# Weight splitting in a two-layer hybrid decoder: the exact parts kept in DRAM by the first token group and loaded by the other three

## The chip, the cores and the metric

The kernel runs on one core of one Trainium2 chip. A time is the device time of one execution in microseconds (us). The time before is 2350.82 us, the median of three runs (2337.67 to 2355.39). Lower is better. TensorE is called PE here, VectorE DVE, ScalarE ACT, GpSimd POOL, and SyncE, which issues the DMAs, SP, as in the profile.

## The reference

The reference is one inference step of a two-layer decoder for 16 meta tokens and 2048 prompt tokens, and for 8 samples of one token each, with a model width of 1024, all in 32-bit floats.

```
# layer 0 (AB): sliding-window attention and gated DeltaNet side by side
h = _rmsnorm(x, norm_g)
proj = jnp.einsum('btd,de->bte', h, w_in)             # 1024 -> 3336
...
mix = jnp.concatenate([oa, ob.reshape(Bn, T, B_VAL)], axis=-1)
y = x + jnp.einsum('bte,ed->btd', mix, w_out)         # 1024 -> 1024
# layer 1 (C): gated linear attention
h = _rmsnorm(x, norm_g)
proj = jnp.einsum('btd,de->bte', h, w_in)             # 1024 -> 3088
...
y = x + jnp.einsum('bte,ed->btd', o.reshape(Bn, T, C_VAL), w_out)
```

Then comes one last RMSNorm. The step also gives back the caches and the states of both layers. Most of the work are the four products of all tokens with weight matrices.

## The kernel before, in words

**Precision.** A 32-bit number is written as the sum of two parts that PE multiplies exactly in its faster format (float32r): `hi` is the rounded number, `lo` is the rest. A product needs three matmuls: hi with hi, hi with lo, lo with hi. Tokens and weights are both taken apart in this way.

**Groups.** The tokens are worked off in four groups (`NGROUPS`): group 0 has the 8 samples, the 16 meta tokens and 512 prompt tokens (536 columns, in two halves of 268), the others have 512 prompt tokens each. Every group goes through both layers, and so every group uses all the weights once. The head of the next group (`ab_head`) is put ahead of the last product of layer C of the group before (`c_out`).

**Weights.** `load_w` (L234) brings one weight tile: SP loads it from DRAM into a tile `raw` (L239), ACT (L244) or, for layer C's values, DVE (L246) writes `hi` into a tile `wh`, and POOL subtracts to give `lo` in a tile `wl` (the subtraction shows under the helper's line L111). A tile of over 512 columns is split in two pieces. There are two buffers of `raw`, three of `wh` and three of `wl`. This is done in each of the four groups anew. `proj` (L370) then multiplies: for each of eight blocks of 128 input features three matmuls of 512 columns (L108), so 24 matmuls for a full weight of 128 x 1024; `proj_tok` (L388) does the same for layer C's values with the tokens as the stationary operand, from two weight tiles at once, and `proj_tok2` (L409) for the attention's values, with both parts side by side in tiles of `wh`. In `c_out` the last group takes the last two feature blocks of the output weights apart in a piece of code of its own (L1205).

**Output products.** `ab_out` multiplies by the first layer's output weights in two passes of eight weight tiles, the first over the features that are ready early (three of eight blocks in the later groups), the second over the rest; each weight of the second pass ends with an addition on DVE and a store to DRAM (L969). `c_out` works in one pass, with a load from DRAM and a store (L1186) for each weight.

**What sets the order.** The program emits the large products (`bulk`) and, between their pieces, steps of the streams of dependent work (attention blocks, the DeltaNet's inverses and scans, norms). An estimated clock with a latency for each step (`DEF_LAT`) says when a stream gets its next step. The instructions then go to the engines' queues; each engine works its queue off in order. A tile's buffer is given to the next tile of its tag when the last reader of the old one is done. All DMAs are issued by SP, in one queue.

Other names in the profile: `pp` are the accumulators of the large products, `pc` those of the streams, `t` any working tile, `inv` the DeltaNet's triangular inverse, `x1d` and `x2d` the residual in DRAM. L114 is the helper for scalar_tensor_tensor on DVE, L118 and L120 those for tensor_scalar, L187 a power on POOL.

Of the kernel before, what the change touches and what calls it, by code (L numbers as in the profile page):

```python
# [9 lines left out]
F32 = mybir.dt.float32  # L10
# [33 lines left out]
def _constants():  # L44
# [9 lines left out]
    # the first level's, transposed  # L54
# [13 lines left out]
def kernel(ctx: ExitStack, tc: tile.TileContext, ins, outs):  # L68
# [12 lines left out]
    def nm(s):  # L81
        cnt[0] += 1
        return f"{s}_{cnt[0]}"
# [47 lines left out]
    UN = 1088  # L131
# [3 lines left out]
    w0 = wp.tile([128, UN], F32, tag="raw", bufs=2, name="raw0")  # L135
# [6 lines left out]
    # The first group's parts are taken before its tokens' scale is known, which then goes to the products.  # L142
# [46 lines left out]
    # W_up, stacked in exact parts  # L189
# [8 lines left out]
    # carried state  # L198
# [15 lines left out]
    # running log decays of the heads as rows, in exact parts, and what picks a head's rows  # L214
    # (the same rows hold layer C's gates in their time)
# [18 lines left out]
    def load_w(src, n, eng):  # L234
        if src is w0:
            raw = w0
        else:
            raw = wp.tile([128, UN], F32, tag="raw", bufs=2, name=nm("raw"))
            SY.dma_start(raw[:, :n], src)  # L239
        hi = wp.tile([128, UN], F32R, tag="wh", bufs=3, name=nm("wh"))  # L240
        lo = wp.tile([128, UN], F32R, tag="wl", bufs=3, name=nm("wl"))
        for w in (slice(0, n // 2), slice(n // 2, n)) if n > 512 else (slice(0, n),):
            if eng == "A":
                A.copy(hi[:, w], raw[:, w])  # L244
            else:
                V.tensor_copy(hi[:, w], raw[:, w])  # L246
            TT(lo[:, w], raw[:, w], hi[:, w].bitcast(F32), sub, G)
        return hi, lo
# [5 lines left out]
    # Streams of dependent work are interleaved with the bulk of the products along an estimated clock (us).  # L254
# [29 lines left out]
    def bulk(gen, hooks=()):  # L284
        # hooks: what to emit at the pieces of the product, counted from its last one
# [14 lines left out]
    # Tiles that live long: a stream asks for room and yields until others have given some back.  # L300
# [69 lines left out]
    def proj(q, src, H, evac, eng="V", kts=tuple(range(8))):  # L370
        # src holds the rows of the input features kts, in that order
        hiX, loX = H
        K = len(kts)
        hi, lo = load_w(src, 128 * K, "A")
# [13 lines left out]
    def proj_tok(q, parts, H, N, windows):  # L388
        hiX, loX = H
        per = 8 // len(parts)  # L390
        hl = [load_w(src, per * N, "V") for src in parts]
# [17 lines left out]
    def proj_tok2(q, src, H, N, windows):  # L409
        # few columns: both parts of the weights side by side in one pass of each part of the tokens  # L410
        raw = wp.tile([128, UN], F32, tag="raw", bufs=2, name=nm("raw"))
        SY.dma_start(raw[:, :8 * N], src)
        ws = []
        for x in range(2):
            w = wp.tile([128, 4, 2, N], F32R, tag="wh", bufs=3, name=nm("wh"))
            r = raw[:, 4 * N * x:4 * N * x + 4 * N].rearrange("p (k m) -> p k m", k=4)
            A.copy(w[:, :, 0], r)
            TT(w[:, :, 1], r, w[:, :, 0].bitcast(F32), sub, G)
            ws.append(w)
        for (slot, c0, evac) in windows:  # L420
# [64 lines left out]
        # sample tokens  # L485
# [36 lines left out]
        # caches of the sample tokens  # L522
# [75 lines left out]
    def ab_proj(q, src, evac):  # L598
        if q.g:
            return proj(q, src, q.H, evac)  # L600
# [5 lines left out]
        return proj(q, src, q.H, ev)  # L606

    def ab_norm(q, ahead):
        # in two steps: the tokens times their scale, ahead of time, then the parts
# [66 lines left out]
    def ab_scalars(q, BA, NS):  # L676
        # token scalars: write strength, log decay and its running sums
# [46 lines left out]
    def ab_k(q):  # L724
# [28 lines left out]
        yield from ab_proj(q, ins["w_ab"][0] if g else w0, ev_k)  # L753
# [9 lines left out]
    def ab_conv(q, h):  # L763
# [23 lines left out]
        for j in range(3):  # L787
# [22 lines left out]
            bulk(ab_proj(q, ins["w_ab"][9 + ct], ev_c))  # L810
# [9 lines left out]
        bulk(ab_proj(q, ins["w_ab"][21 + h], gate(q, G_[0], 4 + h)))  # L820
# [4 lines left out]
    def ab_swa(q, u):  # L825
# [17 lines left out]
        bulk(ab_proj(q, ins["w_ab"][1 + u], ev_q))  # L843
# [4 lines left out]
        bulk(ab_proj(q, ins["w_ab"][5 + u], gate(q, Gt, u)))  # L848
# [80 lines left out]
    def ab_out(q, xs):  # L929
        # output projection, residual; the next layer's input as it comes  # L930
# [903 lines left out]
```

## Time and profile before

| what | value |
|---|---|
| runs, us | 2337.67, 2355.39, 2350.82 |
| span of the profiled execution, first to last instruction | 2346.1 us |
| instructions | 44344 |
| mean granted PE clock | 0.972 |
| read from HBM, written | 192.56 MB, 31.77 MB |
| mean DMA rate over the span | 96 GB/s |

The profile shows one execution. Its own time is given by its span of 2346.1 us alone; the median of the runs is 4.7 us above it. How to read its rows: a group of instructions is named by line, engine, operation and tiles, written tile first (`wl<-raw,wh` is the subtraction that gives `lo`), then the shape and a count; behind the first bar the busy time and the mean duration, behind the second the idle time of the engine ahead of them and who ended it. In a timeline, the first number is the start in us from the span's start, the second the duration; a bracket gives the wait ahead of it and its releaser. The matmuls are pipelined, so that PE's durations overlap. The granted clock is a share of full speed.

### The profile page before, as it was taken

The page shows a single profiled execution, that of the slowest core. Times are in us where ns is not written, and L with a number is a line of the kernel's source. Part 1 is how long each engine was busy: PE and PEld are TensorE (multiplying, and loading weights), DVE is VectorE, ACT ScalarE, POOL GpSimd, SP SyncE. Part 2 cuts the span into 40 slices and gives each one's busy share as a digit, 9 for nine tenths or more (in the row PEclk, how much of TensorE's full clock was granted, in tenths as well). Part 3 has the DMA queues.
Part 4 walks back from the last instruction along what each step waited for, and adds up shares of the span by engine and source line. Part 5 has one row for each costly group of instructions (what it writes and reads, how often), then busy time and mean ns, then how long its engine had stood idle before and what let it go on. Part 6 is the DMA issues. An engine that isn't in the chain of part 4 may idle for free. (4 is left out here: it accounts for less than half of the span.)

```text
span 2346.1 us, 44344 instructions
## 1 busy us (share of the span) xinstructions
PE 2193.5 (93%) x17290; PEld 1834.6 (78%) x17290; DVE 1406.2 (60%) x3708; ACT 1007.8 (43%) x2617; POOL 960.8 (41%) x794
## 2 busy tenths in 40 slices
PE   7898997989999999999999999999999999999998
PEld 6777786988879776778887777778887867778886
DVE  7788974565475666646445666565446475665533
ACT  4444543343463344444444344345344334455333
POOL 2332222444543332345453523255563423254644
PEclk9999998999999999999999999999999999999999
DMA  4221213324533411232333511142323521152223
GB/s 133 81 78 46 64 42 104 107 84 149 171 118 125 161 46 50 83 116 79 107 101 104 184 55 46 53 152 68 109 99 98 163 96 47 35 155 78 84 72 113
DMA packets 108077, 226.15 MB, mean 96 GB/s; under 512 B 15899, under 2 KB 42171, under 8 KB 107851
## 3 DMA queue, kind: packets, MB, share of 16 engines
q1 hardware_dynamic: 107866, 223.31, 30.1%
q8 instruction: 136, 2.23, 0.4%
q14 instruction: 75, 0.61, 0.1%
HBM read 192.56 MB, written 31.77 MB: 96 GB/s over the span
## 5 line engine op out<-in xcount | busy, mean ns | idle before, releaser
L108 PE MATMUL pp<-t,wh 128*128 128x512 f32 (+1 forms) x4528 | 1289.8, 368 | 18.2 <-ACT t L148 8.9
L111 POOL TENSOR_TENSOR wl<-raw,wh 128x512 fp32r<-128x512 f32 (+4 forms) x552 | 702.7, 1292 | 968.1 <-ACT wh L244 808.4
L108 PEld LDWEIGHTS pp<-t,wh 128*128 128x128 f32 x4528 | 794.7, 193 | 132.2 <-issue 13.0
L108 PE MATMUL pp<-t,wl 128*128 128x512 f32 (+1 forms) x2264 | 817.4, 361 | 0.3 <-POOL wl L111 0.3
L108 PEld LDWEIGHTS pp<-t,wl 128*128 128x128 f32 x2264 | 436.1, 193 | 60.3 <-issue 3.2
L244 ACT CAST wh<-raw 128x512 fp32r<-128x512 f32 (+3 forms) x488 | 269.3, 585 | 426.2 <-PE pp L108 178.5
L108 PE MATMUL pp<-wh,t 128*128 128x256 f32 (+1 forms) x1360 | 246.6, 290 | 9.6 <-DVE QKt L111 6.3
L108 PEld LDWEIGHTS pp<-wh,t 128*128 128x128 f32 x1360 | 209.1, 192 | 13.0 <-DVE QKt L111 6.5
L111 POOL TENSOR_TENSOR t<-t,t 128x512 fp32r<-128x512 f32 (+3 forms) x128 | 164.4, 1301 | 122.0 <-ACT t L548 83.1
L114 DVE SCALAR_TENSOR_TENSOR t<-pp,t 128x512 f32<-128x512 f32 (+3 forms) x160 | 92.6, 584 | 124.7 <-PE pp L108 89.2
L187 POOL TENSOR_TENSOR sm<-sm,mh 128x2 f32<-128x2 f32 (+3 forms) x84 | 65.5, 780 | 247.3 <-DVE sm L120 110.2
L108 PE MATMUL pp<-wl,t 128*128 128x256 f32 (+1 forms) x544 | 157.2, 289 | 0.0
L114 DVE SCALAR_TENSOR_TENSOR t<-t,PV,t 128x512 fp32r<-128x512 f32 (+5 forms) x160 | 116.0, 729 | 30.8 <-ACT t L965 22.2
L111 DVE TENSOR_TENSOR t<-t,t 128x512 f32<-128x512 f32 (+4 forms) x103 | 87.4, 852 | 36.0 <-ACT t L367 34.1
L108 PEld LDWEIGHTS pp<-wl,t 128*128 128x128 f32 x544 | 104.9, 193 | 0.7
L114 DVE SCALAR_TENSOR_TENSOR t<-pp,PV,t 128x511 f32<-128x511 f32 (+2 forms) x108 | 79.9, 740 | 17.9 <-ACT t L801 17.8
L108 PEld LDWEIGHTS pc<-t,t 128*128 128x128 f32 (+4 forms) x496 | 64.9, 166 | 29.0 <-ACT t L1462 4.9
L108 PE MATMUL pc<-t,t 128*128 128x128 f32 (+5 forms) x496 | 80.7, 274 | 7.1 <-DVE t L114 4.0
L873 ACT ACTIVATE t<-t,sm 128x257 f32<-128x257 f32 x128 | 64.1, 503 | 29.6 <-DVE sm L114 28.7
L111 DVE TENSOR_TENSOR QKt<-pp,t 128x512 f32<-128x512 f32 (+1 forms) x40 | 23.0, 583 | 87.4 <-PE pp L108 87.4
L114 DVE SCALAR_TENSOR_TENSOR t<-t,t 128x512 f32<-128x512 f32 (+4 forms) x92 | 63.9, 695 | 18.7 <-ACT t L1102 11.7
L111 DVE TENSOR_TENSOR t<-pp,t 128x268 f32<-128x268 f32 (+1 forms) x90 | 44.5, 496 | 49.2 <-PE pp L108 27.0
(336 smaller groups left out, 3006.9 us busy)
## 6 DMA issues: line engine op xcount, KB each, us to landing
raw<-in_w_ab SPq DMA_DIRECT2D x100, 512.0 KB, 3.7
raw<-in_w_c SPq DMA_DIRECT2D x64, 512.0 KB, 3.6
t<-in_xT SPq DMA_DIRECT2D x72, 256.0 KB, 4.0
raw<-in_w_cv SPq DMA_DIRECT2D x24, 512.0 KB, 3.5
raw<-in_w_co SPq DMA_DIRECT2D x24, 512.0 KB, 3.6
out_yp<-t SPq DMA_DIRECT2D x32, 256.0 KB, 2.3
raw<-in_w_abo SPq DMA_DIRECT2D x24, 320.0 KB, 3.2
t<-rows SPq DMA_DIRECT2D x24, 256.0 KB, 4.4
```

The costliest lines, as they stand in the source:

```text
L108: T.matmul(out, lhsT, rhs, start=start, stop=stop)
L111: (eng or V).tensor_tensor(out, a, b, op=op)
L114: V.scalar_tensor_tensor(out, a, s, b, op0=op0, op1=op1)
L187: G.tensor_tensor(out, x, mh[0:x.shape[0]].to_broadcast(list(x.shape)), op=ALU.pow)
L244: A.copy(hi[:, w], raw[:, w])
L873: A.activation(S_[:, kv], S_[:, kv], AF.Exp, bias=st[:, 2 + kv:3 + kv], accum_out=st[:, 4 + kv:5 + kv])
```

## The change

In group 0 a weight is taken apart as before, and both parts are then stored to a DRAM tile of their own (`keep_parts`; the stores are emitted two weights later by `flush`). In groups 1 to 3 `load_w` loads the two parts straight into `wh` and `wl` (`load_parts`), with no work on ACT, DVE or POOL. The same holds for the attention's values (`proj_tok2`) and for the last group's piece in `c_out`. All weight tiles, `raw`, `wh` and `wl` (and `wv`), now share one tag with `NW` = 8 buffers, in place of two, three and three. Each weight gets a name and a column, by which its parts are found again; where the change passes these on (`ab_proj`, the calls of `proj` and `proj_tok`) only arguments differ. Comments are also dropped.

```
+NW = 8
...
+    parts_of = {}
+    unstored = []
+
+    def w_tile(n, dt=F32R):
+        return wp.tile([128, UN], dt, tag="w", bufs=NW, name=nm(n))
+
+    def flush(keep):
+        while len(unstored) > keep:
+            SY.dma_start(*unstored.pop(0))
+
+    def keep_parts(w, n, hi, lo):
+        name, c0 = w
+        if name not in parts_of:
+            parts_of[name] = dr.tile([128, 2, UN], F32, tag=nm("wd"), bufs=1, name=nm("wd"))
+        for x, t in enumerate((hi, lo)):
+            unstored.append((parts_of[name][:, x, c0:c0 + n], t.bitcast(F32)))
+
+    def load_parts(w, n, hi, lo):
+        name, c0 = w
+        flush(0)
+        for x, t in enumerate((hi, lo)):
+            SY.dma_start(t.bitcast(F32), parts_of[name][:, x, c0:c0 + n])
+
+    def load_w(q, w, src, n, eng):
+
+        if q.g:
+            hi, lo = w_tile("wh"), w_tile("wl")
+            load_parts(w, n, hi[:, :n], lo[:, :n])
+            return hi, lo
         if src is w0:
             raw = w0
         else:
-            raw = wp.tile([128, UN], F32, tag="raw", bufs=2, name=nm("raw"))
+            raw = w_tile("raw", F32)
             SY.dma_start(raw[:, :n], src)
-        hi = wp.tile([128, UN], F32R, tag="wh", bufs=3, name=nm("wh"))
-        lo = wp.tile([128, UN], F32R, tag="wl", bufs=3, name=nm("wl"))
-        for w in (slice(0, n // 2), slice(n // 2, n)) if n > 512 else (slice(0, n),):
+        flush(2)
+        hi, lo = w_tile("wh"), w_tile("wl")
+        for c in (slice(0, n // 2), slice(n // 2, n)) if n > 512 else (slice(0, n),):
...
+        keep_parts(w, n, hi[:, :n], lo[:, :n])
         return hi, lo
...
     def proj_tok2(q, src, H, N, windows):
-        raw = wp.tile([128, UN], F32, tag="raw", bufs=2, name=nm("raw"))
-        SY.dma_start(raw[:, :8 * N], src)
+        flat = [w_tile("wv") for _ in range(2)]
+        if q.g:
+            load_parts(("abv", 0), 8 * N, *flat)
+        else:
+            raw = w_tile("raw", F32)
+            SY.dma_start(raw[:, :8 * N], src)
...
             W = []
             for m in range(0, 8, 2):
-                raw = wp.tile([128, UN], F32, tag="raw", bufs=2, name=nm("raw"))
-                SY.dma_start(raw[:, :512].rearrange("p (m k) -> p m k", m=2),
-                             ins["w_co"][m:m + 2, :, 768:1024].rearrange("m p k -> p m k"))
                 hi, lo = ft(F32R, (128, 4, 128)), ft(F32R, (128, 4, 128))
-                A.copy(hi.rearrange("p k m -> p (k m)"), raw[:, :512])
-                TT(lo.rearrange("p k m -> p (k m)"), raw[:, :512], hi.rearrange("p k m -> p (k m)").bitcast(F32), sub, G)
-                W += [(hi[:, 0:2], lo[:, 0:2]), (hi[:, 2:4], lo[:, 2:4])]
+                for i in range(2):
+                    k = slice(2 * i, 2 * i + 2)
+                    load_parts((("co", m + i), 768), 256, *(t[:, k].rearrange("p k m -> p (k m)") for t in (hi, lo)))
+                    W.append((hi[:, k], lo[:, k]))
```

More of the change, by code (lines that the diff above doesn't have):

```diff
@@ L134 @@
     X0 = [ft() for _ in range(8)]
-    w0 = wp.tile([128, UN], F32, tag="raw", bufs=2, name="raw0")
+    w0 = wp.tile([128, UN], F32, tag="w", bufs=NW, name="raw0")
     for kt in range(8):
@@ L237, in load_w @@
         else:
-            raw = wp.tile([128, UN], F32, tag="raw", bufs=2, name=nm("raw"))
+            raw = w_tile("raw", F32)
             SY.dma_start(raw[:, :n], src)
-        hi = wp.tile([128, UN], F32R, tag="wh", bufs=3, name=nm("wh"))
-        lo = wp.tile([128, UN], F32R, tag="wl", bufs=3, name=nm("wl"))
-        for w in (slice(0, n // 2), slice(n // 2, n)) if n > 512 else (slice(0, n),):
+        flush(2)
+        hi, lo = w_tile("wh"), w_tile("wl")
+        for c in (slice(0, n // 2), slice(n // 2, n)) if n > 512 else (slice(0, n),):
             if eng == "A":
-                A.copy(hi[:, w], raw[:, w])
+                A.copy(hi[:, c], raw[:, c])
             else:
-                V.tensor_copy(hi[:, w], raw[:, w])
-            TT(lo[:, w], raw[:, w], hi[:, w].bitcast(F32), sub, G)
+                V.tensor_copy(hi[:, c], raw[:, c])
+            TT(lo[:, c], raw[:, c], hi[:, c].bitcast(F32), sub, G)
+        keep_parts(w, n, hi[:, :n], lo[:, :n])
         return hi, lo
@@ L368, in sq_acc, with proj @@
             TT(acc[:, :q.C], acc[:, :q.C], sq[:, :q.C], add, eng)
-    def proj(q, src, H, evac, eng="V", kts=tuple(range(8))):
+    def proj(q, w, src, H, evac, eng="V", kts=tuple(range(8))):
         hiX, loX = H
         K = len(kts)
-        hi, lo = load_w(src, 128 * K, "A")
+        hi, lo = load_w(q, w, src, 128 * K, "A")
         hi = hi[:, :128 * K].rearrange("p (k m) -> p k m", k=K)
@@ L386, in proj, with proj_tok @@
             yield 3 * 0.000423 * n
-    def proj_tok(q, parts, H, N, windows):
+    def proj_tok(q, w, parts, H, N, windows):
         hiX, loX = H
         per = 8 // len(parts)
-        hl = [load_w(src, per * N, "V") for src in parts]
+        hl = [load_w(q, (w + (x,), 0), src, per * N, "V") for x, src in enumerate(parts)]
         for (slot, c0, evac) in windows:
@@ L409, in proj_tok2 @@
     def proj_tok2(q, src, H, N, windows):
-        raw = wp.tile([128, UN], F32, tag="raw", bufs=2, name=nm("raw"))
-        SY.dma_start(raw[:, :8 * N], src)
+        flat = [w_tile("wv") for _ in range(2)]
[4 more added lines that the diff above has]
+            SY.dma_start(raw[:, :8 * N], src)
         ws = []
         for x in range(2):
[L415 to L418, printed above, removed]
+            w = flat[x].rearrange("p (k y m) -> p k y m", k=4, y=2)
             ws.append(w)
+            if q.g == 0:
+                r = raw[:, 4 * N * x:4 * N * x + 4 * N].rearrange("p (k m) -> p k m", k=4)
+                A.copy(w[:, :, 0], r)
+                TT(w[:, :, 1], r, w[:, :, 0].bitcast(F32), sub, G)
+        if q.g == 0:
+            keep_parts(("abv", 0), 8 * N, *flat)
         for (slot, c0, evac) in windows:
@@ L596, in ab_first, with ab_proj @@
         q.rbn = rstd_row(q, q.rst)
-    def ab_proj(q, src, evac):
+    def ab_proj(q, i, evac):
+        w, src = (("ab", i), 0), w0 if i == 0 and q.g == 0 else ins["w_ab"][i]
         if q.g:
-            return proj(q, src, q.H, evac)
+            return proj(q, w, src, q.H, evac)
         def ev(ps, c0, n):
@@ L605, in ev @@
             evac(u[:, :n], c0, n)
-        return proj(q, src, q.H, ev)
+        return proj(q, w, src, q.H, ev)
     def ab_norm(q, ahead):
@@ L752, in ev_k @@
                 SY.dma_start(outs["kp"], kf)
-        yield from ab_proj(q, ins["w_ab"][0] if g else w0, ev_k)
+        yield from ab_proj(q, 0, ev_k)
     def gate(q, Gt, xcol):
@@ L809, in ev_c @@
                 STT(o, o, 1.0, Tt[:, d:d + m], add, mul)
-            bulk(ab_proj(q, ins["w_ab"][9 + ct], ev_c))
+            bulk(ab_proj(q, 9 + ct, ev_c))
             if h == 0 and j == 0:
@@ L819, in ab_conv @@
         G_.append(ft())
-        bulk(ab_proj(q, ins["w_ab"][21 + h], gate(q, G_[0], 4 + h)))
+        bulk(ab_proj(q, 21 + h, gate(q, G_[0], 4 + h)))
         done.append(1)
@@ L842, in ev_q @@
                 STT(QS[kv][o, d:d + m], ps[r, s:n], 0.125, QS[kv][r, d:d + m].bitcast(F32), mul, sub)
-        bulk(ab_proj(q, ins["w_ab"][1 + u], ev_q))
+        bulk(ab_proj(q, 1 + u, ev_q))
         gx = []
@@ L847, in ab_swa @@
         Gt = ft()
-        bulk(ab_proj(q, ins["w_ab"][5 + u], gate(q, Gt, u)))
+        bulk(ab_proj(q, 5 + u, gate(q, Gt, u)))
         gx.append(1)
@@ L1005, in c_v @@
         if h == 0:
-            yield from proj_tok(q, [ins["w_cv0"][0], ins["w_cv0"][1]], q.H, 272, ws)
+            yield from proj_tok(q, ("cv", h), [ins["w_cv0"][0], ins["w_cv0"][1]], q.H, 272, ws)
             for (src, c0, n) in [(gkp, q.off, 512)] + ([(gkx, 0, EX)] if g == 0 else []):
@@ L1011, in c_v @@
         else:
-            yield from proj_tok(q, [ins["w_cv"][h - 1, 0], ins["w_cv"][h - 1, 1]], q.H, 256, ws)
+            yield from proj_tok(q, ("cv", h), [ins["w_cv"][h - 1, 0], ins["w_cv"][h - 1, 1]], q.H, 256, ws)
         q.VH = VH
```

13 lines of the change are left out of this document (6 added, 7 removed).

## The prediction, written before the run

> **What bounds the kernel now.** I read the page first, then each engine's busy time by stretches of the four groups, then the waits of TensorE (PE).
>
> ```profile
> span 2346.1 us, 44344 instructions
> PE 2193.5 (93%) x17290; PEld 1834.6 (78%) x17290; DVE 1406.2 (60%) x3708; ACT 1007.8 (43%) x2617; POOL 960.8 (41%) x794
> q1 hardware_dynamic: 107866, 223.31, 30.1%
> ```
>
> PE is busy for 93% of the span. No change that leaves the matmuls alone can gain more than its idle 152.6 us and what the clock loses. By stretches (columns: length, then busy us of PE, PEld, DVE, ACT, POOL, then granted PE clock, DMA share, GB/s; the first row is nearly all of group 0, the others are one period of the other groups each):
>
> ```profile
> 0.00:631.00 631.00, 556.46 (x5092) 500.49 (x5093) 432.37 (x1375) 275.17 (x783) 211.97 (x186) 0.95 0.30 94
> 751.00:1293.00 542.00, 520.43 (x3924) 424.30 (x3924) 311.82 (x748) 233.39 (x583) 237.00 (x191) 0.98 0.30 97
> 1293.00:1833.00 540.00, 518.22 (x3848) 418.11 (x3847) 312.71 (x746) 233.28 (x583) 237.92 (x192) 0.98 0.30 97
> 1833.00:2346.10 513.10, 482.21 (x3409) 391.49 (x3407) 278.40 (x667) 211.79 (x527) 220.46 (x185) 0.98 0.30 92
> ```
>
> Half of the idle time, 74.5 us, lies in group 0, whose splitting stays. Each later period has 21 to 31 us of it. Who ends PE's waits from 631 us to the end (total us, times, longest):
>
> ```profile
> PE pc L108 <- DVE inv L111: 19.4, 9, 3.1
> PE pc L108 <- DVE t L111: 15.4, 11, 3.1
> PE pc L108 <- DVE QKt L111: 7.5, 3, 2.5
> PE pc L1490 <- DVE t L114: 6.3, 3, 2.1
> PE pc L108 <- DVE inv L118: 4.7, 4, 1.2
> PE pc L884 <- DVE t L118: 4.2, 9, 0.8
> PE pc L108 <- DVE t L114: 3.2, 3, 1.1
> PE pc L108 <- DVE Tg L114: 2.4, 2, 1.2
> ```
>
> These eight rows come to 63.1 us and all of them name VectorE (DVE). No weight tile is among them. In the whole kernel PE waits for a weight part only here:
>
> ```profile
> PE pp L108 <- ACT wh L244: 1.2, 1, 1.2
> PE pp L108 <- POOL wl L111: 0.3, 1, 0.3
> ```
>
> So the splitting is hidden from PE directly. If the change gains, it gains through DVE.
>
> **Does the splitting make DVE late?** Two runs of the same four DVE operations, and what GpSimd (POOL) did beside the second; then the wait of PE that the second one ends:
>
> ```profile
> 1346.61 1.16 DVE L111 TENSOR_TENSOR inv<-t,CC 32x128 f32<-32x128 f32 x4
> ...
> 1464.61 4.15 DVE L111 TENSOR_TENSOR inv<-t,CC 32x128 f32<-32x128 f32 x4
> ...
> 1464.69 2.65 POOL L111 TENSOR_TENSOR wl<-raw,wh 128x512 fp32r<-128x512 f32 x2 [2.42 <-ACT wh L244]
> 1467.31 1.31 POOL L111 TENSOR_TENSOR t<-t,t 128x512 fp32r<-128x512 f32 x1
> ...
> 1469.63 0.60 PE L108 MATMUL pc<-inv,t 32*32 32x32 f32 x29 [2.51 <-DVE inv L111]
> ```
>
> While POOL subtracts, the DVE work takes 4.15 us in place of 1.16, 2.99 more than it needs, and PE stands for 2.51 us. Two of the three POOL operations beside it are weight splits. A second place, before the sum of squares of layer C's input:
>
> ```profile
> 1566.51 0.43 DVE L246 CAST wh<-raw 128x544 fp32r<-128x544 f32 x1
> 1567.46 1.28 DVE L246 CAST wh<-raw 128x544 fp32r<-128x544 f32 x1
> 1571.09 0.43 DVE L246 CAST wh<-raw 128x544 fp32r<-128x544 f32 x1
> 1572.05 1.28 DVE L246 CAST wh<-raw 128x544 fp32r<-128x544 f32 x1
> ...
> 1575.86 0.35 PE L108 MATMUL pc<-ones,t 128*128 128x1 f32 x2 [2.28 <-DVE t L111]
> ```
>
> Here 3.42 us of casts, which the change takes away in these groups, stand in DVE's own queue ahead of a wait of 2.28 us.
>
> **What is removed.** All work on the tile raw in one period (DVE, ACT, POOL busy us):
>
> ```profile
> 1293.00:1833.00 540.00, 10.43 (x16) 69.08 (x124) 179.89 (x141) 0.98 0.30 97
> ```
>
> Three groups lose about 31 us of DVE, 207 us of ACT and 540 us of POOL. Nothing of this is on PE's path by itself. The parts have the same values and PE issues the same matmuls, so PE's work is 0 either way. What counts is which of PE's waits vanish.
>
> *Waits.* Of the 63.1 us, one wait of 3.1 us belongs to the last token half, which has no splits: 60 us are open. The two waits above go whole (2.51 and 2.28 us are under the 2.99 and 3.42 us of delay). But a wait that vanishes lets PE arrive earlier at the next one, and one POOL operation in three beside the first stays. Bounds: nothing, and all 60. I take 70%, **-42 us**.
>
> *Clock.* After such a wait PE runs slowly for a while (last window: the end of the kernel):
>
> ```profile
> 1467.00:1469.60 2.60, 0.11 (x1) 0.00 (x1) 2.55 (x6) 0.00 (x0) 1.61 (x2) 1.00 0.45 109
> 1469.60:1473.00 3.40, 3.37 (x39) 2.76 (x40) 2.91 (x9) 0.63 (x1) 0.00 (x0) 0.50 0.18 71
> 2330.00:2346.10 16.10, 4.59 (x32) 4.04 (x31) 7.46 (x18) 3.97 (x11) 7.04 (x9) 0.71 0.39 130
> ```
>
> The 3.4 us behind the wait of 2.51 us have clock 0.50, so 1.7 us more are lost. Over the three periods 0.02 x (542 + 540 + 513.1) = 31.9 us are lost to the clock. The end's 0.29 x 16.1 = 4.7 us stay, so 27 are open. With two thirds of the waits gone: **-18 us**. Bounds: 0 and 27. The Trainium skill ("TensorE: Matmul & The Clock Gate", What's actually happening) has the half clock come only after an idle window of about 3.4 us. By that rule waits of 2.5 us cost no clock and the sum lacks this term; the row at 1469.60 speaks against it.
>
> **What is added.** One group's weights are 33,888 KB, 34.7 MB, from these rows and the smaller ones of their kind (issues of four groups, KB each, us to landing):
>
> ```profile
> raw<-in_w_ab SPq DMA_DIRECT2D x100, 512.0 KB, 3.7
> raw<-in_w_abo SPq DMA_DIRECT2D x24, 320.0 KB, 3.2
> raw<-in_w_abo SPq DMA_DIRECT2D x24, 192.0 KB, 2.3
> ```
>
> Stores add 2 x 34.7 MB in group 0, loads 34.7 MB in each later group: 223.3 + 173.5 = 396.8 MB. The page's 223.31 MB at 30.1% of 16 engines' span make 316 GB/s for full engines, so the share becomes 53%. On average this is covered.
>
> *Group 0.* The splits are as before; two stores for each of some 74 loads go through SyncE's queue (SP) and the shared ring of eight tiles holds three tiles per load, so a raw tile comes about one load later than before. Two further weights stand finished while one is multiplied, as before, which covers the 3.7 us of a landing. The stores can delay the samples' small transfers. The trace has no such store. Its nearest row is a 2.7 us wait of PE for a sample transfer (DMA t<-in_kcT); two or three of these more are **+6 us**. Bounds: -5 (another order of issue) and +20.
>
> ```profile
> PE pc L108 <- DMA t<-in_kcT: 2.7, 1, 2.7
> ```
>
> *Groups 1 to 3.* A load takes two of the eight tiles, so four weights are in the ring: a load is issued when the fourth weight ahead of it is used up, three weights before its turn. A 512 KB load lands in 3.7 us, two in a row in some 5.5. PE's pace is 0.69 us for three matmuls:
>
> ```profile
> 1567.15 0.62 PE L108 MATMUL pp<-t,wh 128*128 128x512 f32 x2
> 1567.84 0.62 PE L108 MATMUL pp<-t,wh 128*128 128x512 f32 x2
> ```
>
> A full weight is 24 matmuls or 5.5 us, so three give 16.5 us against 5.5. The tightest place is the first product of ab_out, with 9 matmuls or 2.1 us: 6.2 us against a 2.3 us landing, about 3 for two. **0 us**, hidden behind PE's own matmuls; without that cover each weight would cost the missing part (rival 2).
>
> **Sum.** 2346.1 - 42 - 18 + 6 = 2292 us of span. The median of the runs, 2350.8, is 4.7 us above the profiled span, so I say **2297 us**.
>
> **Rivals.**
>
> 1. *The waits only move.* PE's order of work is fixed with steps spaced by planned latencies; a stream that ends earlier helps only if nothing else ends later. For it: DVE still has some 300 of 540 us of work, and each PE wait is at most 3.1 us. Against it: the 2.99 and 3.42 us are DVE time that disappears. If only a quarter of 60 + 27 comes back: -22 + 6, about **2335 us**.
>
> 2. *PE waits for weights behind SP (the slower side).* SP issues in order. A store of ab_out or c_out that waits for DVE holds the next weight loads back. In groups 1 and 2:
>
> ```profile
> SPq L969 <- DVE t L114: 31.1, 14, 9.0
> SPq L1186 <- DVE t L114: 56.8, 14, 8.8
> ```
>
> Place: the second product of ab_out, 15 matmuls or 3.45 us per weight; three weights are 10.3 us, less about 4 for two landings of 320 KB leaves 6.3 us. SP's mean blocks, 2.2 and 4.1 us, are under this, the longest, 9.0, is over it by 2.7. The point from which it decides is a usual block over 6.3 us. If all 16 weights of this kind in each of three groups (8 in ab_out, 8 in c_out) waited 2.7 us and lost 1.7 to the clock, 48 x 4.4 = 211 us would come on top; with half of them 105: 2297 + 105 = **2402 us**. The Trainium skill ("DMA: Bandwidth & Descriptors", Latency and other measured facts) gives HBM 0.2 us of access on average and 2 us at high load, which speaks against doubling the traffic: by it the spare 6.3 us would shrink to an estimated 4.5, still above the mean blocks; no run here shows that load.
>
> 3. *All of it comes back.* Every wait and the clock: -60 - 27 + 6, **2270 us**. For it: DVE's other slow operations speed up as well.
>
> 4. *The clock does not follow.* Shorter waits that remain still halve it, or the half clock was never theirs (so the rule of the Trainium skill on the clock gate, weighed above): -42 + 6, about **2315 us**.
>
> 5. *The change doesn't act as said*: loads of parts are put behind the last store of a group, or the issue order is worse elsewhere: about **2350 us**.
>
> **How the numbers follow.** Forecast 0.50, rival 1 0.17, rival 2 0.11, rival 3 0.10, rival 4 0.08, rival 5 0.04. The three runs of before lie 0.75% apart, so about 1% (24 us) is what a measurement tells from no change. Faster is forecast, 3 and 4: 0.68. Within 1%: rivals 1 and 5, 0.21. Slower: rival 2, 0.11. Range: the unknowns are the waits (0 to -60), the clock (0 to -27) and group 0 (-5 to +20). Down to **2250** it takes in rival 3 with group 0 at its best and some gain in group 0's waits; up to **2355** rivals 1, 4 and 5. What is left out is rival 2 and a little on either side. The likeliest case alone: 2275 to 2320.
>
> **What the changed profile would show.** Right: no raw tile from group 1 on; POOL about 420 us, ACT 800, DVE 1250 to 1300, since its slow operations shrink too; PE's busy time nearly equal; its waits after 631 us near 25 us and clock 0.99 there; DMA share about 53%. Step by step: casts and stretched inv<-t,CC gone ahead of the waits at the sum of squares and the inverse; no row in which PE waits for a DMA of wh or wl. Wrong: PE waiting for those DMAs (rival 2), the same DVE waits with shorter DVE operations (rival 1), or a first group longer by over 20 us.

## The result, and the profile after

The kernel with the change takes **2285.6 us** (median of four runs, 2280.67 to 2298.03), beside 2349.28 us for four runs of the kernel before taken with it: a ratio of **0.973** (95% interval 0.969 to 0.978). The forecast was 2297 us. Every profile below is one execution; the one of the changed kernel is the slowest of its four runs (2298.03 us, span 2296.2), so its spans are compared with other spans, not with the medians.

The page of the changed kernel:

```profile
span 2296.2 us, 43978 instructions
PE 2181.3 (95%) x17290; PEld 1831.8 (80%) x17290; DVE 1245.8 (54%) x3660; ACT 820.0 (36%) x2241; POOL 422.0 (18%) x370
q1 hardware_dynamic: 162362, 396.84, 50.9%
```

The load that was to go is gone: POOL has lost 539 us, ACT 188, DVE 160, of which only some 31 us were DVE's own casts. PE issues the same 17290 matmuls. The bytes are those worked out (396.8 MB), and they take 50.9% of the DMA engines.

To compare the same work, the next rows cut both kernels at the same matmuls: the first 5000, the next 1000, the last 11,290. Columns as before: length, busy us (instructions) of PE, PEld, DVE, ACT, POOL, then granted clock, DMA share, GB/s. First the changed kernel:

```profile
0.00:640.90 640.90, 556.67 (x5001) 498.49 (x5002) 415.32 (x1366) 269.89 (x771) 205.01 (x179) 0.93 0.53 179
640.90:766.00 125.10, 120.04 (x1002) 101.70 (x1001) 67.23 (x170) 49.26 (x128) 37.82 (x33) 0.95 0.62 214
766.00:2296.20 1530.20, 1504.56 (x11292) 1231.61 (x11290) 763.23 (x2125) 500.86 (x1343) 179.12 (x159) 0.99 0.50 169
```

And the kernel before:

```profile
0.00:618.50 618.50, 543.96 (x5000) 489.63 (x5001) 426.32 (x1366) 269.19 (x771) 204.44 (x180) 0.95 0.29 92
618.50:737.10 118.60, 114.78 (x1002) 97.14 (x1002) 71.39 (x170) 54.53 (x139) 53.52 (x44) 1.00 0.41 131
737.10:2346.10 1609.00, 1534.76 (x11292) 1247.79 (x11290) 908.54 (x2173) 684.10 (x1709) 702.85 (x571) 0.98 0.30 96
```

Read the lengths: **+22.4, +6.5 and -78.8 us**, together the -49.9 us between the two spans. Group 0 has lost time, the other groups have won more than was forecast. In the last row length less busy time gives PE's idle time: 25.6 us after, 74.2 before, so 48.6 us are waits that went. The other 30.2 us are PE's busy time for the same matmuls. Most of that is the clock: added up from the trace's record of the granted clock, 33.8 us are lost to half clock in the last row before and 8.6 us after, 25.2 us less. What the other 5 us are the record does not show.

Of PE's waits there before, the rows that name DVE come to 63.8 us. Who still ends PE's waits there in the changed kernel (total us, times, longest):

```profile
PE pc L109 <- DVE t L112: 5.5, 3, 3.1
PE pc L109 <- DVE t L115: 3.4, 3, 1.2
PE pc L109 <- issue: 2.7, 4, 1.1
PE pc L109 <- DVE inv L112: 2.6, 4, 0.7
```

All rows of this view come to 16.8 us, 11.7 of them name DVE, and none names a weight tile. The two places that the prediction followed now look like this (start, duration, engine: DVE, POOL and PE at the inverse, then DVE and PE at the sum of squares):

```profile
1453.58 2.25 DVE L112 TENSOR_TENSOR inv<-t,CC 32x128 f32<-32x128 f32 x4
...
1454.39 1.29 POOL L112 TENSOR_TENSOR t<-t,t 128x512 fp32r<-128x512 f32 x1 [3.22 <-ACT t L588]
...
1456.70 0.45 PE L109 MATMUL pc<-inv,t 32*32 32x32 f32 x32 [0.62 <-DVE inv L112]
...
1556.40 0.68 DVE L112 TENSOR_TENSOR t<-t,t 128x512 f32<-128x512 f32 x1
...
1558.14 0.95 PE L109 MATMUL pc<-ones,t 128*128 128x1 f32 x8
```

At the inverse the two subtractions are gone; one POOL operation that is no weight split stays beside DVE, so the four DVE operations take 2.25 us (4.15 before, 1.16 undisturbed) and PE waits 0.62 us in place of 2.51. At the sum of squares no cast stands ahead in DVE's queue and PE does not wait at all. But the casts were not the whole delay there. Before, the addition to the sum of squares was stretched as well, beside POOL's splits (the two additions ahead of it took 1.78 and 1.85 us):

```profile
1573.91 1.81 DVE L111 TENSOR_TENSOR t<-t,t 128x512 f32<-128x512 f32 x1
```

Three additions at 0.68 us in place of these make 3.4 us less, as much as the casts, two of which were themselves stretched (1.28 us beside 0.43 for the same shape).

Why DVE has won five times what its casts cost is seen by operands. The same 540 us of each kernel's clock, about one period, operation by operation (busy us, mean ns of one, then idle time before); first before:

```profile
L111 DVE TENSOR_TENSOR t<-t,t 128x512 f32<-128x512 f32 x21 | 22.4, 1065 | 10.9 <-ACT t L367 10.7
L111 DVE TENSOR_TENSOR inv<-t,CC 32x128 f32<-32x128 f32 x16 | 8.4, 523 | 0.2
L114 DVE SCALAR_TENSOR_TENSOR t<-pp,t 128x512 f32<-128x512 f32 x24 | 16.4, 687 | 21.4 <-PE pp L108 20.6 <-DMA t<-in_xT 0.3
L118 DVE TENSOR_SCALAR t<-t,sm 128x256 f32<-128x256 f32 x32 | 12.8, 443 | 0.2
```

then after:

```profile
L112 DVE TENSOR_TENSOR t<-t,t 128x512 f32<-128x512 f32 x26 | 18.0, 693 | 17.2 <-ACT t L400 17.2
L112 DVE TENSOR_TENSOR inv<-t,CC 32x128 f32<-32x128 f32 x16 | 6.5, 408 | 0.2
L115 DVE SCALAR_TENSOR_TENSOR t<-pp,t 128x512 f32<-128x512 f32 x28 | 19.3, 691 | 34.3 <-PE pp L109 15.7 <-DMA t<-x1d 15.6 <-DMA t<-in_xT 2.7
L119 DVE TENSOR_SCALAR t<-t,sm 128x256 f32<-128x256 f32 x32 | 9.8, 350 | 0.2
```

An operation that reads two tiles of SBUF falls from 1065 to 693 ns and from 523 to 408. One of the same size that takes one of its two inputs from an accumulator (`pp`) has 687 and 691: it was never slowed. The Trainium skill ("SBUF — State Buffer", Who interferes with whom) has this rule: a DVE instruction with two SBUF inputs contends with a GpSimd instruction that reads SBUF, one with at most one SBUF input does not, unless it runs in what the Trainium skill calls a 2-port mode. The first three rows agree with it. The last row is an operation on one tile (`sm` holds one number per partition) that falls as well, from 443 to 350 ns; in which mode it ran the trace does not show. So one SBUF tile is not always safe.

### The profile page after: what moved, and what is told of

Same layout as the page of the kernel before. It is cut to its first block, busy times and chain, and to the rows that moved or that the text cites. A ratio compares the mean times of both kernels' runs of the same rounds, so it can differ in the third digit from the quotient of the medians.

```text
span 2296.2 us, 43978 instructions
## 1 busy us (share of the span) xinstructions
PE 2181.3 (95%) x17290; PEld 1831.8 (80%) x17290; DVE 1245.8 (54%) x3660; ACT 820.0 (36%) x2241; POOL 422.0 (18%) x370
## 3 DMA queue, kind: packets, MB, share of 16 engines
q1 hardware_dynamic: 162362, 396.84, 50.9%
## 4 chain that ended last, share of the span: by engine, by line
PE 70%; DVE 4%; DMA 2%; issue 2%; ACT 1%; POOL 1%; SPq 0%; DVEq 0%; POOLq 0%; ACTq 0%
PE pp L109 52%; PE pc L109 14%; DVE t L112 1%; PE pc L925 1%; DVE t L115 1%; DVE inv L112 1%; DMA t<-rows 1%; DMA raw<-in_w_cv 1%; PE pc L1704 0%; POOL wl L112 0%; DMA t<-x2d 0%; PE pc L1483 0%; PE pc L1475 0%; DVE t L1092 0%; PE pc L1672 0%
## 5 line engine op out<-in xcount | busy, mean ns | idle before, releaser
L112 POOL TENSOR_TENSOR wl<-raw,wh 128x512 fp32r<-128x512 f32 (+3 forms) x138 | 177.6, 1304 | 357.4 <-PE pp L109 147.2
L109 PE MATMUL pp<-wh,t 128*128 128x256 f32 (+1 forms) x1088 | 211.3, 290 | 5.0 <-DVE QKt L112 5.0
L109 PEld LDWEIGHTS pp<-wh,t 128*128 128x128 f32 x1088 | 174.2, 192 | 7.2 <-DVE QKt L112 5.2
L115 DVE SCALAR_TENSOR_TENSOR t<-pp,t 128x512 f32<-128x512 f32 (+3 forms) x160 | 93.0, 586 | 146.1 <-PE pp L109 66.0
L115 DVE SCALAR_TENSOR_TENSOR t<-t,PV,t 128x512 fp32r<-128x512 f32 (+5 forms) x160 | 106.4, 670 | 42.1 <-ACT t L1006 25.6
L112 DVE TENSOR_TENSOR t<-t,t 128x512 f32<-128x512 f32 (+4 forms) x103 | 69.8, 681 | 47.6 <-ACT t L400 46.1
L276 ACT CAST wh<-raw 128x512 fp32r<-128x512 f32 (+2 forms) x122 | 68.5, 586 | 69.3 <-DMA raw<-in_w_abo 22.6
L115 DVE SCALAR_TENSOR_TENSOR t<-pp,PV,t 128x511 f32<-128x511 f32 (+2 forms) x108 | 80.2, 743 | 22.6 <-ACT t L842 22.5
L400 ACT ACTIVATE t<-t 128x512 f32<-128x512 f32 (+1 forms) x70 | 44.1, 630 | 91.2 <-DVE t L115 68.9
L112 DVE TENSOR_TENSOR t<-pp,t 128x268 f32<-128x268 f32 (+1 forms) x90 | 44.6, 497 | 54.1 <-PE pp L109 35.8
```

The lines of the kernel that those rows point to most:

```text
L109: T.matmul(out, lhsT, rhs, start=start, stop=stop)
L112: (eng or V).tensor_tensor(out, a, b, op=op)
L115: V.scalar_tensor_tensor(out, a, s, b, op0=op0, op1=op1)
L276: A.copy(hi[:, c], raw[:, c])
L400: A.activation(sq[:, :q.C], x, AF.Square)
```

## The experiments

Two things were open: what makes group 0 slower (the shared ring of eight tiles, the stores' bytes, or the stores' place in SP's queue), and what the later groups live on (POOL freed, the casts gone, or both). Every edit is against the changed kernel. "First part" is the time of the first 5000 matmuls, 618.5 us before and 640.9 after.

### The shared ring alone

All four groups split their weights as before, in the shared ring, with nothing stored or loaded as parts.

```
-        if q.g:
-            hi, lo = w_tile("wh"), w_tile("wl")
-            load_parts(w, n, hi[:, :n], lo[:, :n])
-            return hi, lo
...
-        keep_parts(w, n, hi[:, :n], lo[:, :n])
```

> All four groups split their weights as before; the only change left of the edit is that raw, wh and wl share eight buffers. Before, PE has begun 5000 matmuls (group 0's) after 618.5 us, with the change after 640.9 us; a period of a later group is 541 us before and 512 us with the change. Theory A (group 0 is longer because the shared buffers let a raw tile in one or two loads later, so that ACT's cast and what stands behind it wait): group 0's 5000 matmuls again take about 640 us, the later groups are no shorter than before, the whole is 2365 to 2400 us. Rival B (group 0 is longer because of the stores' traffic): about 618 us, the whole about 2350 us. Rival C (only the order of issue differs by chance): something between.

Measured: 2355.04 us, ratio 1.001 (0.998 to 1.004). The first part, same columns as above:

```profile
0.00:615.40 615.40, 541.07 (x5001) 487.20 (x5002) 413.66 (x1366) 269.44 (x772) 204.15 (x180) 0.95 0.30 92
```

The ring alone costs group 0 nothing and brings the whole nothing.

### No stores

Only the first weight's parts are stored, and every later load of parts fetches these. The loads have their full size, and the later groups multiply by other weights.

```
+        if not parts_of:
+            one = parts_of["one"] = dr.tile([128, 2, UN], F32, ...)
...
-            SY.dma_start(t.bitcast(F32), parts_of[name][:, x, c0:c0 + n])
+            SY.dma_start(t.bitcast(F32), parts_of["one"][:, x, 0:n])
```

> The changed kernel with the parts of the first weight alone stored; all loads of the later groups read these same parts, so they multiply by one weight over and over (the computation is changed), with the same number and size of loads. Theory A (shared buffers): group 0's 5000 matmuls still take about 640 us, the whole about 2285 us. Rival B (stores): about 618 us, the whole about 2262 us.

Measured: 2265.6 us, ratio 0.963 (0.959 to 0.968).

```profile
0.00:614.20 614.20, 537.60 (x5001) 484.52 (x5002) 413.82 (x1366) 269.33 (x772) 203.55 (x180) 0.96 0.30 94
```

The first part is 26.7 us shorter than with the stores (19.9 us beside a second profile of the change, below): they cost group 0 its whole loss. Seven tenths of the 26.7 us, 556.67 - 537.60 = 19 us, appear not as idle time but as longer busy time of PE at a lower clock (0.93 for 0.96). With the stores free the change would be worth about 0.963.

### Separate buffers, with the stores

Two buffers of `raw`, three of `wh` and three of `wl`, as in the kernel before.

```
-        return wp.tile([128, UN], dt, tag="w", bufs=NW, name=nm(n))
+        tag, bufs = {"raw": ("raw", 2), "wl": ("wl", 3)}.get(n, ("wh", 3))
+        return wp.tile([128, UN], dt, tag=tag, bufs=bufs, name=nm(n))
```

> The changed kernel with the buffers as before: two for raw, three for the upper parts, three for the lower parts. Theory A (shared buffers): group 0's 5000 matmuls take about 620 us; the later groups have loads issued two weights ahead instead of three, 11 us against 5.5 us of landing, so a period stays near 512 us; the whole about 2265 us. Rival B (stores): about 640 us and 2286 us. A third view (the later groups need the fourth weight in flight): periods over 520 us and the whole over 2300 us.

Measured: 2293.04 us, ratio 0.975 (0.971 to 0.978), first part 640.6 us. With these buffers three weights are in supply in the later groups, and not four. What that leaves among PE's waits there is one row that the shared ring does not have:

```profile
PE pp L109 <- DMA wl<-wd: 4.5, 3, 1.9
```

One weight less costs 4.5 us of waits in three groups, 1.9 us at the worst place. So the later loads have slack with four weights in supply, and nearly enough with three.

### Stores of 16 columns

As "No stores", but every weight also issues its two stores, each of 16 columns in place of up to 1088: the waits and the order in SP's queue stay, nearly all the bytes go. The later groups multiply by other weights.

```
+        few = dr.tile([128, 2, 16], F32, tag=nm("few"), bufs=1, name=nm("few"))
...
-            unstored.append((parts_of[name][:, x, c0:c0 + n], t.bitcast(F32)))
+            unstored.append((few[:, x], t[:, 0:16].bitcast(F32)))
```

> As the run with the parts of the first weight alone stored (the later groups multiply by that one weight, the computation is changed), but every weight's two parts are now stored by their first 16 columns: as many stores as in the changed kernel, in the same places of SP's queue with the same waits, with next to no bytes. With no stores group 0's 5000 matmuls took 614 us, with all stores 641. Theory B1 (a store stands in SP's queue until its part is cast, and raw tiles and the samples' transfers behind it come late): again about 640 us, the whole near 2286 us. Theory B2 (the stores' bytes fill the DMA engines): about 616 us, the whole near 2265 us.

Measured: 2288.28 us, ratio 0.974 (0.971 to 0.977).

```profile
0.00:631.80 631.80, 544.20 (x5000) 487.67 (x5001) 410.81 (x1366) 270.88 (x772) 204.63 (x180) 0.94 0.32 93
```

Stores with almost nothing in them, at a DMA share of 0.32, still cost 17.6 of the 26.7 us. The times of the whole even put them level with full stores: 22.7 us above the run without stores, where the change, measured twice, lies 20.0 and 23.1 us above it. So the bytes cost little or nothing. SP's own queue shows what such stores do. What SP waited for in the first part, in the changed kernel (L246 is a store, L271 the load of a `raw` tile):

```profile
SPq L271 <- PE pp L109: 102.9, 26, 15.3
SPq L246 <- ACT wh L276: 89.4, 36, 10.4
SPq L246 <- POOL wl L112: 70.8, 40, 6.6
```

with stores of 16 columns (L275 the load):

```profile
SPq L246 <- ACT wh L280: 150.0, 44, 19.6
SPq L275 <- PE pp L109: 92.7, 17, 15.8
SPq L246 <- POOL wl L112: 42.1, 42, 12.1
```

and without stores:

```profile
SPq L271 <- PE pp L109: 283.6, 41, 18.1
```

Without stores SP's long waits for the weights are for a free tile: it runs as far ahead as the ring lets it. With stores it stands 160 or 192 us at the head of a store whose part is not yet written, and whatever comes next, a `raw` load or another transfer, stands behind it; when a load's turn comes its tile is more often free (17 or 26 waits for a tile in place of 41). How this reaches PE is not shown. ACT's casts stood 36.1 us until a `raw` tile landed in the first part of the changed kernel, and 60.1 us in the kernel without stores, so late weights are not seen to be the path.

### The stores on another queue

Three placings: on POOL's queue, on ACT's queue, and each part on its own writer's queue at once (`hi` on ACT, or POOL where DVE writes it, `lo` on POOL, with no delay by two weights).

```
-            SY.dma_start(*unstored.pop(0))
+            G.dma_start(*unstored.pop(0))      # or A.dma_start
```

> The changed kernel with the stores issued from POOL's queue in place of SP's: the same bytes, nothing of them in SP's queue. B1 (SP's queue): group 0's 5000 matmuls about 617 us, the whole 2262 to 2270 us. B2 (bytes): about 640 us and 2286 us. POOL has to issue 148 DMAs, which may stretch DVE's operations in group 0 and hold up its subtractions: then over 640 us.

> The changed kernel with the stores issued from ACT's queue in place of SP's. B1: group 0 gains what SP's queue loses, but a store that waits for POOL's subtraction now stands ahead of ACT's evacuations: 620 to 640 us for 5000 matmuls, the whole 2265 to 2290 us. B2: 640 us or more, 2286 us or more.

> The changed kernel with each part stored at once by the engine that made it, the upper part from ACT's queue right behind its cast, the lower part from POOL's right behind the subtraction (what DVE casts is stored from POOL's queue), so that almost no store waits for another engine. If a waiting store at the head of a queue is the cost: group 0's 5000 matmuls take 616 to 624 us, the whole 2262 to 2276 us. If the issue of a DMA costs the engine's own time: ACT's casts and evacuations come later and the whole is 2280 us or more.

Measured: on POOL's queue 2279.89 us, ratio 0.970 (0.966 to 0.974), first part 624.8; on ACT's 2306.5 us, 0.981 (0.978 to 0.984), first part 656.9; on the writers' queues 2308.3 us, 0.983 (0.980 to 0.986), first part 650.2. The first lies between its two forecasts. The second lies outside the range given for SP's queue as the cause and would fit the bytes, against which the small stores speak. The third has the time of its second branch, in which issuing costs the engine's own time. Both of these are slower than the change. On POOL's queue an issue takes POOL's time. In the first 640 us (DMA issues of POOL, mean ns of one, then the idle time before them by releaser):

```profile
L246 POOL DMA_DIRECT2D wd<-wl x63 | 35.8, 568 | 11.8 <-POOL wl L112 8.9 <-issue 2.9
L246 POOL DMA_DIRECT2D wd<-wh x63 | 35.4, 561 | 59.2 <-ACT wh L276 46.8 <-ACT junk L1485 8.1 <-ACT junk L1518 1.6
```

SP is free again (no wait at a store, and 37 waits of 279.5 us for a free tile), and 71 us of POOL's time and 47 us of its waits for ACT take their place. Why ACT's queue costs most in the first part is not shown. Argued only: an issue that waits in ACT's in-order queue holds up the streams' work behind it.

The change and the best of these were then taken once more, side by side:

> The changed kernel once more, unaltered, as the measure for the two runs beside it: 2280 to 2298 us, ratio 0.973.

> The changed kernel with the stores on POOL's queue, in more rounds: if SP's queue was the cost of group 0, the whole is 2270 to 2282 us and under the changed kernel beside it; if the first result was chance, 2286 us.

Measured: the change 2288.7 us, 0.973 (0.970 to 0.977), first part 634.1; with the stores on POOL's queue 2283.11 us, 0.971 (0.968 to 0.974), first part 623.9. The first part gains 16.1 and 10.2 us in the two pairs, the whole 5.7 and 5.6 us, and the intervals overlap: a likely gain that these runs do not prove. The second run on POOL's queue, 2283.11 us, lies just above the range of 2270 to 2282 us that was to show SP's queue as the cost. The two runs of the change also show the spread of the first part: 640.9 and 634.1 us for one and the same program.

### Stores on POOL's queue with separate buffers

The two edits that each did no harm, together.

```
+        tag, bufs = {"raw": ("raw", 2), "wl": ("wl", 3)}.get(n, ("wh", 3))
...
-            SY.dma_start(*unstored.pop(0))
+            G.dma_start(*unstored.pop(0))
```

> The changed kernel with the stores on POOL's queue and with the buffers of before (two, three and three): raw tiles have buffers that no store holds. Each half alone left the whole at 2280 to 2293 us. If group 0's rest of the loss (624 us for 5000 matmuls with POOL's stores against 614 without stores) comes from buffers held by stores: 615 to 620 us and 2265 to 2277 us; if it is the stores' bytes or POOL's time for issuing them: 624 us or more and 2280 us or more.

Measured: 2301.86 us, ratio 0.980 (0.977 to 0.982), first part 637.8: the second branch of the expectation, the bytes or POOL's time. SP's queue in the first part (L272 and L239 are the load of a `raw` tile), here and then in the kernel before:

```profile
SPq L272 <- POOL wl L112: 326.9, 54, 20.3
```

```profile
SPq L239 <- POOL wl L111: 324.6, 55, 20.4
```

SP waits just as it did before, and no store stands in its way; the first part is 19.3 us longer than before all the same. So SP's queue is not the only way to lose this time: what is left here are the bytes and some 70 us of POOL's time for the issues. The loss has another form too. It is all idle time of PE, 94.1 us for 74.5 before, with PE's busy time as before (543.7 and 544.0 us); in the changed kernel more than half of the loss is busy time. With two `raw` buffers the loads run no further ahead than before; that the lead which the shared ring gives is what covers the stores in the run of 624.8 us is argued, not shown.

### The later groups: POOL's work kept

In groups 1 to 3 POOL adds each lower part to itself in place, in the pieces of the old subtraction. The lower parts are doubled.

```
+            for c in (slice(0, n // 2), slice(n // 2, n)) if n > 512 else (slice(0, n),):
+                TT(lo[:, c], lo[:, c].bitcast(F32), lo[:, c].bitcast(F32), add, G)
```

> The changed kernel, but in the later groups POOL adds every lower part to itself in place, one operation of the size of the old subtraction for each (the lower parts are doubled, so the product differs slightly). Nothing is cast on ACT or DVE. Theory (the later groups gain because POOL no longer stretches DVE's operations): most of the gain goes, a period is 530 us or more, PE's waits for DVE after 650 us are over 40 us, the whole 2330 to 2350 us. Rival (the gain is from the casts taken off ACT and DVE): a period stays near 515 us, the whole under 2300 us.

Measured: 2331.09 us, ratio 0.992 (0.990 to 0.995): most of the net gain is gone. (Group 0 still pays for its stores here, so what is gone of the later groups' own gain is less; see below.)

### The later groups: the casts kept

In groups 1 to 3 ACT (or DVE, where it did so before) casts each upper part in place. The values stay.

```
+            for c in (slice(0, n // 2), slice(n // 2, n)) if n > 512 else (slice(0, n),):
+                if eng == "A":
+                    A.copy(hi[:, c], hi[:, c].bitcast(F32))
+                else:
+                    V.tensor_copy(hi[:, c], hi[:, c].bitcast(F32))
```

> The changed kernel, but in the later groups ACT (for layer C's values DVE) casts the loaded upper part in place again, which changes no value; POOL has no subtraction. POOL's work alone brought the whole from 2286 to 2331 us. Theory (DVE's stretched operations are most of the gain, the casts the rest): 2290 to 2305 us. Rival (ACT's casts cost as much): 2315 us or more.

Measured: 2299.99 us, ratio 0.978 (0.975 to 0.981). The stretch of the same last 11,290 matmuls, to where PE's last long run ends, one row per kernel: before, POOL's work kept, casts kept, and the change.

```profile
737.10:2338.30 1601.20, 1534.31 (x11291) 1247.64 (x11290) 906.46 (x2167) 683.73 (x1708) 701.45 (x569) 0.98 0.30 95
```

```profile
768.70:2319.90 1551.20, 1513.47 (x11292) 1237.05 (x11290) 827.48 (x2119) 500.24 (x1342) 589.52 (x561) 0.99 0.49 166
```

```profile
764.10:2292.40 1528.30, 1505.54 (x11292) 1229.50 (x11290) 778.31 (x2167) 679.65 (x1698) 177.37 (x157) 1.00 0.50 168
```

```profile
766.00:2287.00 1521.00, 1503.41 (x11289) 1230.76 (x11287) 761.15 (x2119) 500.49 (x1342) 177.72 (x157) 1.00 0.50 169
```

Of the 80.2 us between the first row and the last, POOL's work brings back 30.2 and the casts 7.3; 42.7 are given by neither alone. The 7.3 us are of one profile, and the interval of that run overlaps with the change's. Nor are these the old waits only. Each of the two kernels has one large row among PE's waits that the kernel before hardly has, here first with POOL's work kept, then with the casts kept:

```profile
PE pc L109 <- POOL rs L188: 9.1, 4, 3.0
```

```profile
PE pc L109 <- ACT t L932: 5.2, 6, 2.5
```

Before, PE waited 1.0 us for POOL's `rs` and not for this ACT operation. The rows that name DVE come to 63.8 us before, 24.7 with POOL's work kept, 11.5 with the casts kept and 11.7 with the change. The stand-in is too light, and this is visible: its operation on 128x512 takes 1101 ns and the old subtraction took 1368,

```profile
L111 POOL TENSOR_TENSOR wl<-raw,wh 128x512 fp32r<-128x512 f32 x301 | 405.7, 1368 | 516.1 <-ACT wh L244 422.1 <-issue 44.8 <-DVE wh L246 27.3
```

```profile
L112 POOL TENSOR_TENSOR wl<-wl 128x512 fp32r<-128x512 f32 x304 | 328.8, 1101 | 557.2 <-DMA wl<-wd 468.6 <-PE pp L109 40.8 <-PE pc L109 22.9
```

and DVE is stretched by less. DVE's busy time in the rows is 906 before, of which 31 are its casts, so 875 against 761 undisturbed: 114 us of stretch. With POOL's stand-in it is 827 - 761 = 66 us, 58% of that. Were the price in proportion, POOL's real work would be worth some 52 us (an estimate), and the open part would shrink to about 21. The waits speak against plain proportion: with 58% of the stretch only 13.0 of the 52.1 us of waits for DVE are back. The stand-in also runs when a load has landed and no longer when a cast is done, so it can fall beside other DVE operations. With all of the splitting back, in the run of the shared ring alone, the whole gain is gone.

One suspicion can be dropped. Before, ACT stood 294 us ahead of casts in its in-order queue, half of it until PE gave a tile free and half with no releaser that the profile shows; with the casts kept it stands nearly as long at casts whose weight has not landed. Before, then with the casts kept:

```profile
ACT wh L244 <- issue: 149.8, 39, 11.9
ACT wh L244 <- PE pp L108: 144.5, 68, 6.7
```

```profile
ACT wh L268 <- DMA wh<-wd: 283.5, 136, 9.0
```

That second kernel is only 7.3 us longer here than the change, so blocking of this size in ACT's queue is cheap in these groups, though the 5.2 us of waits for ACT above may come from it.

## Why the prediction was right, point by point

**The mechanism held in the main.** The gain comes through DVE and not through PE's own waits for weights: 52.1 us of PE's waits for DVE went (63.8 to 11.7). POOL's work kept alone brings back more than the casts kept alone, 30.2 and 7.3 us, though part of the 30.2 us goes by waits for POOL itself. This is the step "If the change gains, it gains through DVE". At its second place the prediction named the casts alone as the delay; by the rows shown above half of the delay there was the stretch of the additions.

**The waits, -42 us, were sized well:** 48.6 us went. The share taken, 70% of 60, was too careful; about 80% went. Of the two waits that were to go whole, the one at the sum of squares did and the one at the inverse left 0.62 us. A wait that vanished did not come back at the next place, so rival 1 falls.

**The clock, -18 us, was sized too small:** by the trace's record of the granted clock 25.2 us came back, near the bound of 27. PE's busy time for the same matmuls fell by 30.2 us. Rival 4 falls. Over the four rows of the last experiment PE's idle time (length less busy) is 66.9, 37.7, 22.8 and 17.6 us and its busy time 1534.3, 1513.5, 1505.5 and 1503.4: both fall together, by about 0.6 us of busy time for each us of waiting; the record of the clock has 29.9, 10.1, 3.8 and 4.0 us lost in them. In the first row half clock comes in 14 stretches of 3.41 or 6.83 us, each behind 3.41 us in which PE was idle for 1.0 to 3.0 us; in the last row there are two (apart from the stretch at each kernel's very end). But waits of 2.25 to 2.50 us were followed by none in four places, the wait at the sum of squares among them, so 0.6 us is an average and no price of a single wait. The Trainium skill ("TensorE: Matmul & The Clock Gate", What's actually happening) lets the clock drop only after an idle window of about 3.4 us; no wait of the kernel before in these groups was longer than 3.1 us, so these rows do not agree with it. The Trainium skill ("TensorE: Matmul & The Clock Gate", A second HAM failure mode: psum-queue depth-cycling) also tells of a kernel in which brief, frequent idling makes the clock swing; that is nearer to them.

**Group 0, +6 us, was the step that failed:** it lost 22.4 us in the first part and 6.5 us in the next, over the bound of +20 (15.6 us in the first part of the second profile). The prediction asked whether stores delay the samples' small transfers, and took its price from a wait for `in_kcT`. That wait did grow, and is a small part:

```profile
PE pc L109 <- DVE inv L112: 11.6, 9, 2.0
PE pc L925 <- ACT wh L276: 10.7, 1, 10.7
PE pc L109 <- DVE t L115: 8.6, 5, 4.1
PE pp L109 <- ACT t L149: 8.2, 2, 7.5
...
PE pc L109 <- DMA t<-in_kcT: 4.9, 1, 4.9
```

What the stores hold up is SP: a store waits for a part of two weights before, and SP goes no further. No store at all, and small stores, show that it is the stores and hardly their bytes; stores on POOL's queue win back 10 to 16 us. Which of PE's waits grows by it stays open: the large products wait only 1.8 us for weight parts, and three of the four longest rows have their like without stores too (13.0 us for `ACT wh` at the place of the 10.7); the fourth, for the `t` of L115, has 8.6 us for 0.3 without stores and 6.4 in the kernel before. The prediction had a blocked SP in its hand, as rival 2, and put it in the wrong group: it saw SP held by the residual's stores in the later groups, where three weights of slack cover it, and not by the weights' own stores in group 0, which the change itself adds with a wait each. That the two stores of each load pass SP's queue was counted as issue alone. It also held that a shared ring would make `raw` come one load later: the ring alone cost nothing.

**The weights of groups 1 to 3, 0 us, held.** No wait of PE names a weight tile there in the changed kernel, at 0.50 DMA share, and with the smaller separate buffers they make 4.5 us in all. Rival 2 falls. Rival 5 falls for the later groups, where the ring and the order of the loads cost nothing that can be seen; its other half, that the issue order is worse elsewhere, is what happened in group 0, at a far smaller price than it named.

**So the size of the sum was luck: two errors of opposite sign.** The later groups gave 78.8 us where 60 were forecast, nearly all that rival 3 asked for (87); group 0 took 28.9 where 6 were forecast. -54 and -49.9 us of span come near each other; the median lay a little further down, since the profiled run is the slowest of four.

**The marks set for the profile:** POOL 422 (about 420), ACT 820 (800), DVE 1246 (1250 to 1300), no `raw` tile in the later groups but the left-over of group 0 (POOL 8.57 us), waits below the 25 us expected, DMA share 50.9% for 53%. One mark of "wrong" also came true, a first group longer by over 20 us, and it was the right alarm for the one step that failed.

**What stays open.** 43 of the 80 us in the later groups are given neither by POOL's stand-in nor by the casts; that the stand-in is too light is measured, that its shortfall is the whole of the rest is not. In group 0 the path from SP's queue to PE is open. The share of the bytes, 9 of 27 us by the first part with small stores and nothing by the times of the whole, is hardly larger than the 6.8 us by which one program's first part differs between two profiles, and the run with POOL's stores and separate buffers lost 19 us with no store in SP's queue. And the same idle time goes with more or less busy time of PE in group 0 (84 us of idle with 556.67 us busy in the one profile of the change, 85 with 549 in the other): the clock lost 44.4 and 35.8 us there, but why it fell more often in the one is not shown.

## What to carry to other kernels

Work that is "hidden" on a side engine can still set the pace: here 540 us of GpSimd's two-input operations and the casts that fed them, none on PE's path, cost some 80 us. The waits that went were nearly all for VectorE, whose operations that read two SBUF tiles had been stretched. Look for it by comparing the mean duration of one operation with and without the other engine beside it, and compare operations with an accumulator as input as a control. When a change adds stores to an in-order queue that also issues loads, price the wait of each store and what is queued behind it, not only its bytes: nearly empty stores cost two thirds of what full ones did in group 0, and all of it by the times of the whole.

## What the hardware showed that was not expected

PE's short waits cost about half as much again in clock: between the kernel before and the change 49.3 us of idle and 25.9 us of clock went together, with no single wait over 3.1 us. Doubling the DMA traffic (0.30 to 0.50 of the DMA engines, 95 to 169 GB/s) made no matmul of the later groups wait for a weight in the changed kernel. And the queue that issues a store matters as much as the store: with no stores the first part took 614.2 us, and the same stores gave one of 624.8 and 623.9 us from POOL's queue, 640.9 and 634.1 from SP's and 656.9 from ACT's, where an issue on POOL takes 561 to 568 ns of that engine.
